# Working on a sublayer's end in two streams of 128 tokens, in the part of the program that handles the latents alone

## The chip, the cores and the metric

The kernel runs on one core of a Trainium2 chip. The time is the device time of one execution in microseconds (us): the median of three runs of the kernel before is 2366.17 us (2364.31 to 2366.91).

## The reference, cut to what matters

Two layers of a backbone work on 256 context tokens and 256 latent tokens, with 1024 channels each. Every layer has three sublayers: a half-step SwiGLU network, four token mixers whose outputs are merged and projected, and a second half-step SwiGLU network. Only the latents are returned, so in the last layer the contexts are needed up to the mixers' inputs and are then dropped.

```python
def rms_norm(x, g):
    y = xf * lax.rsqrt(jnp.mean(xf * xf, axis=-1, keepdims=True) + EPS)
    return (y * g.astype(jnp.float32)).astype(x.dtype)

def ffn_sublayer(x, mod, j, g_pre, g_post, w1, w3, w2):
    h = modulate(rms_norm(x, g_pre), mod[:, :, 3 * j], mod[:, :, 3 * j + 1])
    return x + FFN_RES_WEIGHT * mod[:, :, 3 * j + 2] * rms_norm(swiglu(h, w1, w3, w2), g_post)
...
x_lat = x_lat + mod_lat[:, :, 5] * rms_norm(y_lat, norm_post[layer, 1])
x_lat = ffn_sublayer(x_lat, mod_lat, 2, *ffn_b)
```

Between two sublayers stands, for every token, a norm over the 1024 channels of the first one's output (over all its blocks), the addition to x, and the norm over the sum that the next one begins with.

## The kernel before, in words

Channels lie on the 128 partitions, in 8 blocks, and tokens lie along the free dimension: columns 0 to 255 are the contexts and 256 to 511 the latents. Weights come from memory in pieces of 128 x 1024 (8 blocks of 128 x 128). ScalarE rounds each piece to a high part (`whi`, line 317), VectorE takes the rest as the low part (`wlo`, line 318), and `mm3` (lines 345 to 347) multiplies with three matmuls per block, high by high, high by low and low by high, in the type fp32r. Raw pieces have 3 buffers, split ones 4.

`halves(toks)` lists the streams that lie within a range of tokens: contexts and latents for all 512, and one stream of 256 when the latents are alone. Its callers decide by that list how an end is worked on:

- `post_block` (line 569) takes one finished block of 128 channels: its square, its scaled copy, and, where another sublayer follows, the product with x and the square of the copy. It adds these to three running sums (`sqa`).
- `norms` (line 595) sums them over the partitions with matmuls by a column of ones (`st`, line 303), takes two inverse roots with short VectorE operations (lines 291 to 296), and spreads each over the partitions with a matmul and a copy (`rb`, `rbs`, lines 310 and 312).
- `lead` (line 624) scales the output, adds it to x, and makes the next input `hh`, `hl` block by block (lines 631, 632, 563, 565, 566).
- `turn` (line 636) orders an end. With two streams the last five weight pieces (`skew` = 5) are first used for the first stream, then the norms of that stream are emitted, then the pieces are used for the second stream: four of them still lie split in their buffers, and the first one is loaded and split again. After it come the first stream's `lead`, the second stream's `norms`, the first four pieces of the next sublayer (`ahead`), and the second stream's `lead`. With one stream nothing is held back: all pieces are used for all 256 tokens, and norms and lead follow.
- `ffn` and `mix` read the same list. With two streams, `ffn` runs its first four pieces one stream after the other, and `down` makes separate matmuls for the two streams in the last three output blocks (`m >= KB - 3`). `mix` always uses `halves(ALL_T)` for its own beginning.

The latents are alone from the end of layer 1's mixers (`mix(1, LAT_T, ...)`) through the last network (`ffn(1, 1, LAT_T, ...)`). All engines run the instructions of their queue in order. That order is settled when the program is built, from priorities that follow the order of emission.

Of the kernel before, what the change touches and what calls it, by code (L numbers as in the profile page):

```python
# [7 lines left out]
F32 = mybir.dt.float32  # L8
F32R = mybir.dt.float32r
I32 = mybir.dt.int32  # L10
AF = mybir.ActivationFunctionType
ALU = mybir.AluOpType
# [3 lines left out]
P = 128  # L16
D = 1024
# [8 lines left out]
CTX_T = (0, NCTX)  # L26
LAT_T = (NCTX, NTOK)
# [159 lines left out]
class Kern:  # L187
# [97 lines left out]

    def rsqrt(self, v, shape, tag):
        nc = self.nc
        s = self.small.tile(shape, I32, tag=tag + "s", name=self.nm("rs"))
        y = self.small.tile(shape, F32, tag=tag + "y", name=self.nm("ry"))
        t = self.small.tile(shape, F32, tag=tag + "t", name=self.nm("rt"))  # L290
        nc.vector.tensor_scalar(s, v.bitcast(I32), 1, None, op0=ALU.logical_shift_right)
        nc.vector.tensor_scalar(y.bitcast(I32), s, -1, 0x5F3759DF, op0=ALU.mult, op1=ALU.add)
        for _ in range(3):
            nc.vector.tensor_tensor(t, y, y, op=ALU.mult)
            nc.vector.scalar_tensor_tensor(t, t, -0.5, v, op0=ALU.mult, op1=ALU.mult)
            nc.vector.scalar_tensor_tensor(y, t, 1.5, y, op0=ALU.add, op1=ALU.mult)
        return y
# [177 lines left out]


    def halves(self, toks):
        return [(v, t) for v, t in ((0, CTX_T), (1, LAT_T)) if t[0] >= toks[0] and t[1] <= toks[1]]

    def new_h(self):  # L480
        return [(self.u("hh", F32R, "h"), self.u("hl", F32R, "h")) for _ in range(KB)]
# [87 lines left out]
    def post_block(self, l, s, m, ps, toks, nxt, tag="u"):  # L569

        nc = self.nc
        a, b = toks
        out = self.post
        gp = self.mod[l][3 * s + 2]
        if m not in out["y"]:
            out["y"][m] = self.u("ay")
        y = out["y"][m]

        def add(k, f):
            new = k not in out  # L580
            if new:
                out[k] = self.u("sqa")
            t = out[k] if m == 0 else self.u("sq", tag=tag)
            f(t[:, a:b])
            if m:
                nc.vector.tensor_tensor(out[k][:, a:b], out[k][:, a:b], t[:, a:b], op=ALU.add)  # L586

        add("yy", lambda t: nc.scalar.activation(t, ps[:, a:b], AF.Square))  # L588
        for v, (p, q) in self.halves(toks):
            nc.scalar.activation(y[:, p:q], ps[:, p:q], AF.Identity, scale=gp[:, m, v : v + 1])  # L590
        if nxt:
            add("xa", lambda t: nc.vector.tensor_tensor(t, self.x[m][:, a:b], y[:, a:b], op=ALU.mult))
            add("aa", lambda t: nc.scalar.activation(t, y[:, a:b], AF.Square))

    def norms(self, post, nxt, half):


        nc = self.nc
        v, (a, b) = half
        n = (b - a) // P  # L600

        st = self.ps("st", "h")
        self.stat(st, 0, post["yy"], (a, b))
        if nxt:
            s2 = self.ps("st", "f")
            self.stat(s2, 0, post["aa"], (a, b))
            self.stat(s2, n, post["xa"], (a, b))
        t = self.small.tile([P, n], F32, tag=f"sv{n}", name=self.nm("sv"))
        nc.vector.tensor_scalar(t, st[:, :n], 1.0 / D, EPS, op0=ALU.mult, op1=ALU.add)
        r = self.rsqrt(t, [P, n], f"sr{n}")  # L610
        rs = self.u("rbs", tag="f")
        self.cast(r, n, rs, 0)
        if nxt:
            w = self.small.tile([P, n], F32, tag=f"sx{v}", name=self.nm("sx"))
            nc.vector.tensor_tensor(w, s2[:, :n], r, op=ALU.mult)
            nc.vector.scalar_tensor_tensor(w, s2[:, n : 2 * n], 2.0, w, op0=ALU.mult, op1=ALU.add)
            nc.vector.tensor_tensor(w, w, r, op=ALU.mult)
            nc.vector.scalar_tensor_tensor(w, w, 1.0 / D, self.sx[v], op0=ALU.mult, op1=ALU.add)
            self.sx[v] = w
            r2 = self.rsqrt(w, [P, n], f"sr{n}")  # L620
            self.cast(r2, n, rs, n * P)
        return rs

# [1197 lines left out]
```

## Time and profile before

| | |
|---|---|
| median of 3 runs | 2366.17 us |
| profiled execution | 2369.64 us, of which the span is 2367.8 us |
| TensorE busy, share of the span | 96% |
| VectorE, ScalarE busy | 69%, 38% |
| granted TensorE clock, mean | 0.982 |

The span runs from the first to the last instruction that the profiler recorded; the rest of the profiled execution lies around it. Busy times of TensorE count pipelined matmuls from issue to a modelled end. The start times of two neighbours give their distance.

### The profile page before, as it was taken

The numbers are of one execution on the slowest core, as the hardware profiler recorded it, in microseconds if no ns is written. First come the engines' busy times: TensorE is split into PE (matmuls) and PEld (weight loads), VectorE is DVE, ScalarE is ACT, GpSimd is POOL, SyncE is SP. The second block draws the span as 40 slices with busy tenths as digits, with TensorE's granted clock in tenths as the row PEclk, the third lists the DMA queues.
The fourth block names the chain that finished last, engine by engine and source line by source line (L and its number), as shares of the span: only waits on it lengthen the run. The fifth ranks groups of instructions, "written<-read, shape, count | busy, mean of one in ns | idle before, by whom it ended". The sixth has DMA issues, their size and how long they took to land.

```text
span 2367.8 us, 39296 instructions
## 1 busy us (share of the span) xinstructions
PE 2267.1 (96%) x15428; PEld 1915.7 (81%) x15428; DVE 1635.8 (69%) x4025; ACT 903.0 (38%) x1551; POOL 53.3 (2%) x116
## 2 busy tenths in 40 slices
PE   7999999999999999989999999999998999998997
PEld 4778789987567777878887898888897877898997
DVE  5887675756665574899875478777666886777554
ACT  3322323454443323532332333323244563345442
POOL 0000020000000000000002000000000000000000
PEclk9999999999999999999999999999998999998999
DMA  7545554231541243245554325665532331454663
GB/s 244 172 153 165 184 180 130 75 94 55 171 139 41 85 148 94 72 134 165 180 187 153 98 77 176 180 182 182 182 103 91 113 107 57 161 174 135 185 182 114
DMA packets 105848, 326.82 MB, mean 138 GB/s; under 512 B 16256, under 2 KB 19072, under 8 KB 105664
## 3 DMA queue, kind: packets, MB, share of 16 engines
q1 hardware_dynamic: 97312, 306.52, 42.1%
q0 software_dynamic: 4032, 9.93, 1.2%
q10 hardware_dynamic: 4320, 7.87, 1.0%
q8 instruction: 121, 1.98, 0.3%
q14 instruction: 63, 0.52, 0.1%
HBM read 311.20 MB, written 15.17 MB: 138 GB/s over the span
## 4 chain that ended last, share of the span: by engine, by line
PE 84%; DVE 10%; ACT 3%; DMA 2%; issue 1%; SPq 0%; DVEq 0%; ACTq 0%
PE h L345 11%; PE h L347 11%; PE h L346 11%; PE y L345 6%; PE y L347 6%; PE y L346 6%; PE pj L345 5%; PE pj L347 5%; PE pj L346 5%; PE s L841 2%; DVE wlo L318 2%; DMA araw<-in_w_adaT_dram 1%; PE od L868 1%; ACT whi L317 1%; PE tk L347 1%
## 5 line engine op out<-in xcount | busy, mean ns | idle before, releaser
L317 ACT CAST whi<-raw 128x1024 fp32r<-128x1024 f32 x402 | 421.2, 1050 | 810.4 <-DMA raw<-in_ffn_dram 282.9
L318 DVE TENSOR_TENSOR wlo<-raw,whi 128x1024 fp32r<-128x1024 f32 x402 | 490.7, 1222 | 287.6 <-ACT whi L317 285.5
L345 PE MATMUL h<-hh,whi 128*128 128x512 f32 (+1 forms) x1472 | 528.1, 360 | 12.2 <-DVE gf L686 5.0
L347 PE MATMUL h<-hh,wlo 128*128 128x512 f32 (+1 forms) x1472 | 526.0, 359 | 8.7 <-DVE wlo L318 8.7
L346 PE MATMUL h<-hl,whi 128*128 128x512 f32 (+1 forms) x1472 | 525.7, 358 | 0.0
L345 PEld LDWEIGHTS h<-hh,whi 128*128 128x128 f32 x1472 | 281.8, 192 | 57.6 <-issue 5.3
L347 PEld LDWEIGHTS h<-hh,wlo 128*128 128x128 f32 x1472 | 281.8, 192 | 51.1 <-DVE wlo L318 8.8
L346 PEld LDWEIGHTS h<-hl,whi 128*128 128x128 f32 x1472 | 282.1, 192 | 38.7
L345 PE MATMUL y<-gh,whi 128*128 128x256 f32 (+1 forms) x902 | 290.4, 322 | 2.5 <-ACT t L685 2.5
L347 PE MATMUL y<-gh,wlo 128*128 128x256 f32 (+1 forms) x902 | 291.0, 323 | 0.0
L346 PE MATMUL y<-gl,whi 128*128 128x256 f32 (+1 forms) x902 | 290.5, 322 | 0.0
L345 PE MATMUL pj<-hh,whi 128*128 128x256 f32 (+1 forms) x800 | 276.8, 348 | 3.3 <-ACT hh L565 2.7
L347 PE MATMUL pj<-hh,wlo 128*128 128x256 f32 (+1 forms) x800 | 274.5, 345 | 4.3 <-DVE wlo L318 4.3
L346 PE MATMUL pj<-hl,whi 128*128 128x256 f32 (+1 forms) x800 | 275.7, 346 | 0.4 <-issue 0.4
L345 PEld LDWEIGHTS y<-gh,whi 128*128 128x128 f32 x902 | 171.7, 190 | 15.7 <-ACT t L685 2.7
L347 PEld LDWEIGHTS y<-gh,wlo 128*128 128x128 f32 x902 | 171.7, 190 | 12.9
L346 PEld LDWEIGHTS y<-gl,whi 128*128 128x128 f32 x902 | 171.7, 190 | 12.9
L347 PEld LDWEIGHTS pj<-hh,wlo 128*128 128x128 f32 x800 | 154.2, 194 | 24.7 <-DVE wlo L318 4.9
L345 PEld LDWEIGHTS pj<-hh,whi 128*128 128x128 f32 x800 | 154.2, 194 | 23.6 <-issue 5.2
L346 PEld LDWEIGHTS pj<-hl,whi 128*128 128x128 f32 x800 | 154.5, 194 | 18.4 <-issue 3.9
L424 DVE SCALAR_TENSOR_TENSOR aj<-araw,cr 128x512 f32<-128x512 f32 x112 | 77.0, 687 | 55.9 <-DMA araw<-in_w_adaT_dram 55.7
L586 DVE TENSOR_TENSOR sqa<-sqa,sq 128x256 f32<-128x256 f32 (+1 forms) x154 | 71.6, 493 | 49.9 <-ACT sq L588 49.3
(395 smaller groups left out, 3073.5 us busy)
## 6 DMA issues: line engine op xcount, KB each, us to landing
raw<-in_ffn_dram SPq DMA_DIRECT2D x267, 512.0 KB, 3.8
araw<-in_w_adaT_dram SPq DMA_DIRECT2D x104, 512.0 KB, 4.1
raw<-in_win_dram SPq DMA_DIRECT2D x102, 512.0 KB, 3.7
araw<-in_w_ada_dram SPq DMA_DIRECT2D x24, 512.0 KB, 4.0
raw<-in_wout_dram SPq DMA_DIRECT2D x17, 512.0 KB, 3.5
raw<-in_wbr_dram SPq DMA_DIRECT2D x16, 512.0 KB, 3.6
araw<-in_w_ada_dram SPq DMA_DIRECT2D x22, 256.0 KB, 5.6
s5G<-s5g POOLq DMA_DIRECT2D x16, 256.0 KB, 3.0
```

The source lines that it names most:

```text
L317: self.nc.scalar.copy(hi, src)
L318: self.nc.vector.tensor_tensor(lo, src, hi.bitcast(F32), op=ALU.subtract)
L345: mm(ps, wh, xh, start=start, stop=False, skip_group_check=True)
L346: mm(ps, wh, xl, start=False, stop=False, skip_group_check=True)
L347: mm(ps, wl, xh, start=False, stop=stop, skip_group_check=True)
L424: nc.vector.scalar_tensor_tensor(w if v else junk, w, 1.0, S[v], op0=ALU.mult, op1=ALU.mult, accum_out=t[:, 2 * op + i, v : v + 1])
L586: nc.vector.tensor_tensor(out[k][:, a:b], out[k][:, a:b], t[:, a:b], op=ALU.add)
L841: nc.tensor.matmul(s[:, :w], q[:, j * P : (j + 1) * P], k[:, :w], start=True, stop=True)
L868: nc.tensor.matmul(out[n][64 * h : 64 * h + 64, j * P : (j + 1) * P], vh(kb), ph[:, kb * P : (kb + 1) * P], start=kb == 0, stop=kb == nk - ...
```

## The change

`halves` gives two streams of 128 tokens where the range begins at the latents. `post_block` no longer uses it for choosing the context's or the latent's scale. The small tiles of `norms` and `rsqrt` are made at least two columns wide and cut to the width in use, and the second norm's running sum `sx` is read by the stream's own column.

```diff
     def halves(self, toks):
-        return [(v, t) for v, t in ((0, CTX_T), (1, LAT_T)) if t[0] >= toks[0] and t[1] <= toks[1]]
+
+        mid = (LAT_T[0] + LAT_T[1]) // 2
+        parts = ((1, (LAT_T[0], mid)), (1, (mid, LAT_T[1]))) if toks[0] >= LAT_T[0] else ((0, CTX_T), (1, LAT_T))
+        return [(v, t) for v, t in parts if t[0] >= toks[0] and t[1] <= toks[1]]
...
         add("yy", lambda t: nc.scalar.activation(t, ps[:, a:b], AF.Square))
-        for v, (p, q) in self.halves(toks):
+        for v, (p, q) in ((0, (a, min(b, LAT_T[0]))), (1, (max(a, LAT_T[0]), b))):
+            if p >= q:
+                continue
             nc.scalar.activation(y[:, p:q], ps[:, p:q], AF.Identity, scale=gp[:, m, v : v + 1])
...
-        t = self.small.tile([P, n], F32, tag=f"sv{n}", name=self.nm("sv"))
+        t = self.small.tile([P, 2], F32, tag="sv2", name=self.nm("sv"))[:, :n]
         nc.vector.tensor_scalar(t, st[:, :n], 1.0 / D, EPS, op0=ALU.mult, op1=ALU.add)
-        r = self.rsqrt(t, [P, n], f"sr{n}")
+        r = self.rsqrt(t, [P, n], "sr2")
...
-            w = self.small.tile([P, n], F32, tag=f"sx{v}", name=self.nm("sx"))
+
+            w = self.small.tile([P, 2], F32, tag=f"sx{v if n == 2 else 0}", name=self.nm("sx"))[:, :n]
+            old = self.sx[v] if n == 2 else self.sx[v][:, (a - LAT_T[0]) // P : (a - LAT_T[0]) // P + 1]
...
-            nc.vector.scalar_tensor_tensor(w, w, 1.0 / D, self.sx[v], op0=ALU.mult, op1=ALU.add)
-            self.sx[v] = w
+            nc.vector.scalar_tensor_tensor(w, w, 1.0 / D, old, op0=ALU.mult, op1=ALU.add)
+            if n == 2:
+                self.sx[v] = w
```

## Rows read from the trace of the kernel before

**Rows 1.** The page: busy time of each engine, share of the span, instructions.
```profile
PE 2267.1 (96%) x15428; PEld 1915.7 (81%) x15428; DVE 1635.8 (69%) x4025; ACT 903.0 (38%) x1551; POOL 53.3 (2%) x116
```
**Rows 2.** Windows around mix(1)'s end and the program's end: engines' busy time, clock, DMA.
```profile
core 0: us, PE busy (x) PEld busy (x) DVE busy (x) ACT busy (x) POOL busy (x), PEclk, DMA share, GB/s
2146.00:2166.00 20.00, 9.93 (x46) 9.03 (x45) 17.67 (x64) 6.19 (x13) 0.00 (x0) 0.57 0.19 56
2166.00:2180.00 14.00, 14.00 (x119) 14.00 (x119) 8.45 (x13) 8.37 (x12) 0.00 (x0) 1.00 0.43 117
2180.00:2260.00 80.00, 80.00 (x669) 80.00 (x668) 44.57 (x57) 37.59 (x56) 0.00 (x0) 1.00 0.64 187
2355.00:2368.00 13.00, 1.32 (x6) 0.97 (x5) 7.41 (x28) 0.37 (x1) 0.00 (x0) 0.55 0.24 81
```
**Rows 3.** Timeline of TensorE at mix(1)'s end: start, duration, line, operation [idle, releaser].
```profile
2145.85 0.28 PE L346 MATMUL wo<-ml,whi 128*128 128x256 f32 x1
2145.97 0.28 PE L347 MATMUL wo<-mh,wlo 128*128 128x256 f32 x1
...
2161.58 1.01 PE L345 MATMUL h<-hh,whi 128*128 128x256 f32 x3 [1.52 <-ACT hh L565]
...
2164.96 0.41 PE L345 MATMUL h<-hh,whi 128*128 128x256 f32 x1
2165.17 0.32 PE L346 MATMUL h<-hl,whi 128*128 128x256 f32 x1
2165.33 0.28 PE L347 MATMUL h<-hh,wlo 128*128 128x256 f32 x1
```
**Rows 4.** Timeline of TensorE, two places: 512 columns, then four narrow matmuls of 2 columns.
```profile
526.26 0.39 PE L345 MATMUL pj<-hh,whi 128*128 128x512 f32 x1
526.49 0.39 PE L346 MATMUL pj<-hl,whi 128*128 128x512 f32 x1
...
526.94 1.04 PE L787 MATMUL hs<-cst,sq 128*128 128x2 f32 x8
527.85 0.48 PE L345 MATMUL pj<-hh,whi 128*128 128x512 f32 x1
```
**Rows 5.** Timeline of TensorE: 128 columns in f32, then transposes of 128 columns.
```profile
1874.95 1.13 PE L810 MATMUL hb<-cst,he 128*128 128x128 f32 x8 [0.15 <-DVE he L805]
1875.83 0.36 PE L345 MATMUL pj<-hh,whi 128*128 128x256 f32 x1
...
2101.95 1.06 PE L1578 MATMUL yt<-cst,gl 128*128 128x128 f32 x8
2102.77 0.36 PE L345 MATMUL pj<-hh,whi 128*128 128x256 f32 x1
```
**Rows 6.** Weight loads by shape: count, busy us, mean ns of one, idle before.
```profile
L346 PEld LDWEIGHTS wo<-ml,whi 128*128 128x128 f32 x168 | 31.9, 191 | 1.0
L787 PEld LDWEIGHTS hs<-cst,sq 128*128 128x128 f32 x64 | 8.0, 191 | 2.1 <-ACT sq L900 0.8 <-issue 0.8 <-ACT sq L1205 0.3
L1578 PEld LDWEIGHTS yt<-cst,gl 128*128 128x128 f32 x16 | 1.8, 140 | 0.4 <-issue 0.3
```
**Rows 7.** Timeline at the end of layer 0's mixers, where two streams run: ScalarE, VectorE, TensorE.
```profile
990.16 0.38 ACT L588 ACTIVATE sq<-wo 128x256 f32<-128x256 f32 x1 [1.68 <-PE wo L347]
...
1016.08 1.22 DVE L318 TENSOR_TENSOR wlo<-raw,whi 128x1024 fp32r<-128x1024 f32 x1
...
1017.35 0.58 PE L347 MATMUL h<-hh,wlo 128*128 128x256 f32 x1 [6.52 <-DVE wlo L318]
...
1021.57 0.38 PE L345 MATMUL h<-hh,whi 128*128 128x256 f32 x1
...
1029.93 1.31 ACT L565 ACTIVATE hh<-ht,mod 128x256 fp32r<-128x256 f32 x3 [0.55 <-DVE ht L563]
```
**Rows 8.** VectorE and ScalarE operations by shape, 256 against 128 columns.
```profile
L586 DVE TENSOR_TENSOR sqa<-sqa,sq 128x256 f32<-128x256 f32 x112 | 43.8, 420 | 41.2 <-ACT sq L588 40.8
L1132 DVE TENSOR_TENSOR cx<-cx,ck 128x128 f32<-128x128 f32 x20 | 5.7, 286 | 0.7 <-ACT cx L1130 0.4
L588 ACT ACTIVATE sq<-y 128x256 f32<-128x256 f32 x25 | 9.5, 381 | 46.8 <-PE y L347 46.8
L1130 ACT ACTIVATE cx<-cx 128x128 f32<-128x128 f32 x20 | 6.0, 301 | 3.6 <-DVE cx L1127 3.5
```
**Rows 9.** Timeline of the program's end: TensorE, VectorE, SyncE.
```profile
2353.25 0.28 PE L347 MATMUL y<-gh,wlo 128*128 128x256 f32 x1
2354.55 0.58 PE L303 MATMUL st<-cst,sqa 128*128 128x1 f32 x4 [1.03 <-DVE sqa L586]
2360.40 4.83 SPq L1797 DMA_DIRECT2D out_dram<-x  x8
```
**Rows 10.** DMA issues: source, count, KB each, median us to landing.
```profile
raw<-in_ffn_dram SPq DMA_DIRECT2D x267, 512.0 KB, 3.8
```
**Rows 11.** The page's costliest groups: weight splits, count, busy us, mean ns, idle before.
```profile
L317 ACT CAST whi<-raw 128x1024 fp32r<-128x1024 f32 x402 | 421.2, 1050 | 810.4 <-DMA raw<-in_ffn_dram 282.9
L318 DVE TENSOR_TENSOR wlo<-raw,whi 128x1024 fp32r<-128x1024 f32 x402 | 490.7, 1222 | 287.6 <-ACT whi L317 285.5
```

More of the change, by code (lines that the diff above doesn't have):

```diff
@@ L287, in rsqrt @@
         nc = self.nc
-        s = self.small.tile(shape, I32, tag=tag + "s", name=self.nm("rs"))
-        y = self.small.tile(shape, F32, tag=tag + "y", name=self.nm("ry"))
-        t = self.small.tile(shape, F32, tag=tag + "t", name=self.nm("rt"))
+        w, full = shape[-1], shape[:-1] + [max(shape[-1], 2)]
+        s = self.small.tile(full, I32, tag=tag + "s", name=self.nm("rs"))[..., :w]
+        y = self.small.tile(full, F32, tag=tag + "y", name=self.nm("ry"))[..., :w]
+        t = self.small.tile(full, F32, tag=tag + "t", name=self.nm("rt"))[..., :w]
         nc.vector.tensor_scalar(s, v.bitcast(I32), 1, None, op0=ALU.logical_shift_right)
@@ L617, in norms @@
             nc.vector.tensor_tensor(w, w, r, op=ALU.mult)
-            nc.vector.scalar_tensor_tensor(w, w, 1.0 / D, self.sx[v], op0=ALU.mult, op1=ALU.add)
-            self.sx[v] = w
-            r2 = self.rsqrt(w, [P, n], f"sr{n}")
+            nc.vector.scalar_tensor_tensor(w, w, 1.0 / D, old, op0=ALU.mult, op1=ALU.add)
+            if n == 2:
+                self.sx[v] = w
+            r2 = self.rsqrt(w, [P, n], "sr2")
             self.cast(r2, n, rs, n * P)
```

## The prediction

> **What bounds the kernel now.** The page comes first: TensorE is busy 96% of the span, VectorE 69% [rows 1]. For a kernel so full of matmuls, the question for any edit is how many matmul passes it adds and how much TensorE idle time it fills. Windows come next, laid over the two stretches that the change touches: the end of layer 1's mixers and the program's end. In the steady stretch from 2180 to 2260 TensorE is busy 80.00 of 80 us; from 2146 to 2166 it is busy 9.93 of 20 at a granted clock of 0.57; from 2355 to 2368 it is nearly empty [rows 2]. These two holes are all that a second stream could fill.
>
> The timeline gives the first hole its size. The last mixer projection starts at 2145.97. The first matmul of the next network starts at 2161.58, and until 2165.33 the passes come at 0.21 us instead of 0.12: the clock's lower level, 1.2 GHz, after the wait [rows 3]. Seventeen of the 96 passes of the first four pieces (4 pieces x 8 blocks x 3) start before 2165.33. The other 79 follow at 0.12, so the 96 are issued by 2165.33 + 79 x 0.12 = 2174.8. Without a hole they would be issued by 2146.09 + 96 x 0.12 = 2157.6. **The hole costs 17.2 us.** The second hole is the tail: the span ends 2367.8 - 2353.25 = 14.5 us after the last matmul starts [rows 9].
>
> **What the change adds on TensorE.** Where a matmul of 256 columns becomes two of 128, the number of passes doubles. Counted from the code:
> - mix(1): the last five of eight output blocks, 5 x 8 x 3 = 120 passes become 240.
> - the last network's first four pieces: 96 become 192.
> - its down projection: the blocks m = 5, 6, 7 with 22 inputs each, 3 x 22 x 3 = 198 become 396.
>
> That is 414 extra passes, all in stretches where TensorE is otherwise back to back. So the price of a pass decides. A pass of 256 columns takes 0.12 us [rows 3]; three of 512 take 0.68 from 526.26 to 526.94, 0.227 each [rows 4]: 256 more columns cost 0.107 us, and streaming alone would let 128 columns take 0.120 - 0.053 = 0.067. But each pass also loads 128 columns of weights. That load is recorded at 191 ns for the fp32r pass (`wo`) and the same 191 ns for the f32 pass (`hs`), and at 140 for a transpose [rows 6]. What such a load costs when hardly anything streams is seen in `hs`, 2 columns wide: four f32 matmuls, recorded as eight passes, take from 526.94 to 527.85, 0.114 us a pass [rows 4]. So the load, not the stream, is the floor. From the other side, f32 passes of exactly 128 columns (`hb`) take 0.88 / 8 = 0.110 by their neighbours' starts and (1.13 - 0.28) / 7 = 0.121 by their own span [rows 5]. The trace before has no fp32r pass under 256 columns. I take 0.117, the middle of 0.114 and 0.121, since both rows have the same 191 ns load; outer ends are 0.067 (the load hides) and 0.23 (the narrow fp32r matmul needs two passes, as an f32 one does). **A pass of half the width thus costs what the full one costs**: each split adds 2 x 0.117 - 0.120 = 0.114 us, and 414 of them 47.2 us (44.7 to 50.5 within the inner ends).
>
> The first stream's norms now run between matmuls instead of in the hole: at mix(1) 3 sums and 2 spreads, at the end 1 and 1. At two passes each these are 14 passes of 0.12, **1.7 us**.
>
> A stated rule speaks for a lower price. The Trainium skill, page "TensorE: Matmul & The Clock Gate", section "Back-to-back issue gap", gives about 81 ns per matmul for streams of weight load and matmul at 128 columns; by it 414 x (0.162 - 0.120) = 17.4 us stand in place of 47.2. The rows of 0.110 to 0.121 speak against it here, though no run so far shows this pass itself.
>
> **What it takes away at mix(1).** The first stream's work is over 120 half passes before the second's, so its norms and lead can run under 120 x 0.117 + 1.2 = 15.2 us of matmuls. How long they take is seen where the two streams already run, at the end of layer 0's mixers: the first stream's last evacuation starts at 990.16, and the next network's first matmul only at 1017.35, 27.2 us later. It waited for `wlo` of the next network's first piece, which stands on VectorE behind that stream's lead and the other's post blocks [rows 7]. In that time VectorE does 8 x 4 operations of lead, 5 x 4 of the second stream's blocks and about 4 of the first's last block. At 128 columns each is shorter by 420 - 286 = 134 ns [rows 8], together 56 x 0.134 = 7.5 us; weight splits and the short root operations keep their length. So 27.2 - 7.5 = 19.7 us stand against 15.2 of cover: a wait of 4.5 us, after which the clock is low again. There the 20 passes from 1017.35 to 1021.57 took 4.2 us instead of 2.4 [rows 7], so 1.8 us more. **What remains of the hole: 6.3 us** (bounds 0 and the old 17.2). At the second boundary the second stream's `hh` came 12.6 us after the first matmul in layer 0 [rows 7], here some 2.1 less (16 operations of lead); the 96 half passes last 11.2, and the slow clock's 1.8 adds to that: no wait.
>
> **What it takes away at the end.** The second stream's tail has half the columns: 16 operations of lead save 16 x 0.134 = 2.1 us, square and sum 0.08 + 0.13 [rows 8], sums and spreads two passes less each, 0.5 us, and the copy 0.07. That is **2.9 us** of 14.5; it falls to nothing if the eight output transfers, spaced over 4.83 us now [rows 9], set the end.
>
> **What hides.** The first of the five pieces is loaded and split once more in each end: 3.8 us to landing [rows 10], then 1.05 on ScalarE and 1.22 on VectorE [rows 11]. It waits for one split buffer, free when the second stream's first piece is done (24 x 0.117 = 2.8 us), and is needed after four (11.2 us). On SyncE's queue it stands ahead of the next network's pieces, which are used at half the old pace there. Without that cover it would cost up to 6 us each time. The extra operations of the second stream's post blocks (4 on VectorE, 3 on ScalarE per block) fit into 2.8 us of matmuls per piece. The second root chain, some 30 short operations, lies under the first stream's matmuls at mix(1) and beside the second stream's matmuls at the end. The tiles cut to width and the new loop in `post_block` issue the same instructions elsewhere, at no cost.
>
> **The sum.** 47.2 + 1.7 - 17.2 + 6.3 - 2.9 = **+35.1 us**. The profiled execution's own time is 2369.6, so 2404.7 for it; the median shown is 3.5 us lower, and on it the change gives 2366.2 + 35.1 = **2401 us**. Within the inner ends of the pass and 2 to 11 us of remaining wait the sum goes from +28 to +43, 2394 to 2409.
>
> **Rivals.**
> - *The load hides.* TensorE loads weights for the next pass under the present one, and nothing in the 256-column rows shows the load as a limit. The transposes have a shorter load and come every 0.82 / 8 = 0.10 us [rows 5]. At 0.10 the sum is 414 x 0.080 + 1.7 - 17.2 + 6.3 - 2.9 = +21; at 0.067 it is -6, 2360: faster. It decides below 2p = 0.149, a pass of 0.075. Against it: `hs` pays 0.114 with nothing to stream, and its load is recorded as long as the fp32r one. By the 81 ns of the Trainium skill's page "TensorE: Matmul & The Clock Gate" ("Back-to-back issue gap") this rival's time would be 2371.
> - *The second stream covers nothing.* VectorE is full under the matmuls, as in layer 0, and the hole returns whole at the boundary: +35.1 + 10.9 = +46, 2412. For it speaks that `wlo` stands last in the queue; against it, that the operations are a third shorter.
> - *The narrow fp32r matmul falls back to two passes*, as f32 has them: 414 x (0.46 - 0.12) + 1.7 - 17.2 - 2.9 = +122, 2488. No row shows a narrow fp32r pass, so it can't be excluded; the wait would then be fully covered. Nothing speaks for it either: a 256-column fp32r matmul is one pass at full rate.
>
> **How the numbers follow.** Forecast 0.70, load hides 0.12, no cover 0.10, two passes 0.08. The range of 2380 to 2416 holds nearly all of the forecast and of the second rival, and the dearer quarter of the first: 0.8. A difference of 0.2% is 4.7 us, what a measurement of this kernel can tell. Faster by more comes only from the cheap half of the first rival, 0.06; within it 0.03; slower 0.91.
>
> **What would show it.** `wo`, `h` and `y` matmuls of 128 columns after 2120, 828 of them, at a spacing of 0.114 to 0.121: below 0.075 the forecast fails with its sign, at 0.23 with its size. Between the last `wo` and the first `h` a TensorE wait of 2 to 8 us in place of 15.5, released by a `wlo` or by `hh`. The first `h` no earlier than 2161, since wo itself lasts 14 us longer. From the last `y` to the end 11 to 13 us. Up to 2120 nothing should move by more than a microsecond; if it does, the order of the program has changed elsewhere.

## The result: slower by 3.2%, twice the forecast's loss, and the profile after

The changed kernel takes 2443.44 us (median of 4 runs, 2438.43 to 2448.05), the kernel before beside it 2366.54: a ratio of 1.0315, with a 95% interval of 1.0299 to 1.0330, or +75 us (+71 to +78). Forecast were +35 and 2401 us, with a range that ended at 2416. The sign was right and the size was not.

The page gives the engines' busy time, share and instructions, to be read against [rows 1]:

```profile
PE 2354.7 (96%) x15842; PEld 2001.8 (82%) x15842; DVE 1651.4 (68%) x4137; ACT 912.0 (37%) x1585; POOL 53.3 (2%) x116
```

TensorE has 15842 - 15428 = 414 recorded instructions more, the number counted, and stays 96% busy. What the 414 don't explain is how long they took. The windows over the changed stretches show it (busy time and instructions of TensorE, weight loads, VectorE, ScalarE, GpSimd, then granted clock, DMA share, GB/s), beside [rows 2]:

```profile
2135.60:2148.00 12.40, 12.40 (x113) 12.40 (x113) 9.77 (x27) 7.18 (x20) 0.00 (x0) 1.00 0.55 171
2151.00:2176.70 25.70, 25.30 (x119) 25.13 (x119) 18.47 (x75) 10.37 (x26) 0.00 (x0) 0.50 0.26 81
2176.70:2220.70 44.00, 43.57 (x204) 43.22 (x204) 17.69 (x69) 10.49 (x21) 0.00 (x0) 0.50 0.15 48
2220.70:2224.00 3.30, 3.30 (x22) 3.30 (x22) 1.98 (x3) 1.35 (x2) 0.00 (x0) 0.69 0.02 9
2224.00:2230.00 6.00, 6.00 (x53) 6.00 (x52) 2.99 (x4) 2.69 (x4) 0.00 (x0) 1.00 0.55 178
2376.50:2407.50 31.00, 31.00 (x281) 31.00 (x279) 7.65 (x10) 7.52 (x14) 0.00 (x0) 1.00 0.23 74
2411.40:2434.00 22.60, 22.60 (x109) 22.60 (x107) 4.76 (x18) 1.85 (x4) 0.00 (x0) 0.50 0.00 0
```

The reader is to look at TensorE's busy time and at the clock together. From 2151 to 2220 TensorE is busy for 68.9 of 69.7 us, and the clock is 0.50 throughout, the lower of its two levels, 1.2 GHz. The same happens from 2411 to 2434. From 2376 to 2407 equally narrow passes run at 1.00. A busy TensorE thus says nothing of the pace: 281 instructions in 31 us at one level, 109 in 22.6 at the other.

TensorE's timeline (start, duration, line, operation, idle time before and its releaser) shows where the clock falls and where it returns:

```profile
2148.79 0.28 PE L347 MATMUL wo<-ml,whi 128*128 128x128 f32 x1
2148.91 0.28 PE L348 MATMUL wo<-mh,wlo 128*128 128x128 f32 x1
2149.54 0.38 PE L304 MATMUL st<-cst,sqa 128*128 128x1 f32 x2 [0.36 <-DVE sqa L590]
...
2150.58 0.61 PE L304 MATMUL st<-cst,sqa 128*128 128x1 f32 x4 [0.15 <-DVE rs L292]
2151.04 0.42 PE L347 MATMUL wo<-ml,whi 128*128 128x128 f32 x1
2151.26 0.42 PE L348 MATMUL wo<-mh,wlo 128*128 128x128 f32 x1
...
2176.51 0.41 PE L348 MATMUL wo<-mh,wlo 128*128 128x128 f32 x1
2176.73 0.41 PE L346 MATMUL h<-hh,whi 128*128 128x128 f32 x1
...
2220.53 0.41 PE L348 MATMUL h<-hh,wlo 128*128 128x128 f32 x1
2220.75 0.52 PE L346 MATMUL h<-hh,whi 128*128 128x256 f32 x1
...
2222.56 0.38 PE L348 MATMUL h<-hh,wlo 128*128 128x256 f32 x1
2222.78 0.29 PE L346 MATMUL h<-hh,whi 128*128 128x256 f32 x1
2222.90 0.28 PE L347 MATMUL h<-hl,whi 128*128 128x256 f32 x1
...
2407.49 0.27 PE L348 MATMUL y<-gh,wlo 128*128 128x128 f32 x1
2408.12 0.38 PE L304 MATMUL st<-cst,sqa 128*128 128x1 f32 x2 [0.36 <-DVE sqa L590]
...
2410.88 0.79 PE L311 MATMUL rb<-cst,ry 128*128 128x128 f32 x2 [1.20 <-DVE ry L297]
2411.32 0.45 PE L347 MATMUL y<-gl,whi 128*128 128x128 f32 x1
...
2433.97 0.41 PE L348 MATMUL y<-gh,wlo 128*128 128x128 f32 x1
2435.08 0.59 PE L304 MATMUL st<-cst,sqa 128*128 128x1 f32 x2 [0.69 <-DVE sqa L590]
```

A narrow pass takes 0.111 us before the first sum (as do the 279 y passes from 2376.49 to 2407.49), and 0.213 from 2151.04 on. It stays at 0.213 for 69.7 us, until the first passes of 256 columns: nine of these come at 0.21, the next at 0.12. At the last network's end, ten passes behind the first sum still come fast; the clock falls around the wait of 1.20. In the kernel before, too, the clock had fallen in the hole [rows 3], but what followed it was 256 wide, and it was back within 4 us.

In time, between landmarks of the two profiled executions (before / after, us; of the kernel before, the first pass of a stretch is counted back at 0.12 from its last):

| stretch | before | after | difference |
|---|---|---|---|
| five wo blocks and the wait, to the first h | 29.9 | 41.1 | +11.2 |
| first four h pieces | 13.2 | 44.0 | +30.8 |
| h and y of 256 columns | 154.8 | 155.7 | +0.9 |
| last three y blocks | 23.6 | 57.5 | +33.8 |
| last y to the end of the span | 14.5 | 12.1 | -2.4 |

That is +74.3. The span's other 4.0 lie ahead of the first stretch, where the two programs do the same work. It begins at 2135.7 here, but in two experiments below at 2131.6 and 2131.8, as before (2131.7), and in run 6, which is the kernel before up to there, the last wo comes 2.9 late: the 4 us are a spread between executions. The forecast's sign that nothing up to 2120 would move by more than a microsecond can't be read from single profiles.

### The profile page after: what moved, and what is told of

It is laid out like the page before. It is cut to its first block, busy times and chain, and to the rows that moved or that the text cites. A ratio compares the mean times of both kernels' runs of the same rounds, so it can differ in the third digit from the quotient of the medians.

```text
span 2446.1 us, 40283 instructions
## 1 busy us (share of the span) xinstructions
PE 2354.7 (96%) x15842; PEld 2001.8 (82%) x15842; DVE 1651.4 (68%) x4137; ACT 912.0 (37%) x1585; POOL 53.3 (2%) x116
## 4 chain that ended last, share of the span: by engine, by line
PE 78%; DVE 13%; DMA 5%; ACT 2%; issue 2%; DVEq 0%; ACTq 0%
PE h L346 9%; PE h L348 9%; PE h L347 9%; PE y L348 6%; PE y L346 6%; PE y L347 6%; PE pj L346 5%; PE pj L348 5%; PE pj L347 5%; DVE wlo L319 3%; DMA araw<-in_w_adaT_dram 2%; PE s L850 2%; DMA raw<-in_ffn_dram 1%; ACT whi L318 1%; PE wo L347 1%
## 5 line engine op out<-in xcount | busy, mean ns | idle before, releaser
L346 PE MATMUL h<-hh,whi 128*128 128x512 f32 (+2 forms) x1504 | 544.8, 363 | 10.8 <-DVE gf L695 5.1
L348 PE MATMUL h<-hh,wlo 128*128 128x512 f32 (+2 forms) x1504 | 543.5, 362 | 7.9 <-DVE wlo L319 7.9
L347 PE MATMUL h<-hl,whi 128*128 128x512 f32 (+2 forms) x1504 | 542.7, 362 | 0.0
L347 PEld LDWEIGHTS h<-hl,whi 128*128 128x128 f32 x1504 | 296.5, 197 | 38.7
L346 PE MATMUL y<-gh,whi 128*128 128x256 f32 (+2 forms) x968 | 312.9, 323 | 2.5 <-ACT t L694 2.5
L348 PE MATMUL y<-gh,wlo 128*128 128x256 f32 (+2 forms) x968 | 313.6, 324 | 0.0
L347 PE MATMUL y<-gl,whi 128*128 128x256 f32 (+2 forms) x968 | 313.1, 323 | 0.0
L346 PEld LDWEIGHTS y<-gh,whi 128*128 128x128 f32 x968 | 189.3, 196 | 15.6 <-ACT t L694 2.7
L347 PEld LDWEIGHTS y<-gl,whi 128*128 128x128 f32 x968 | 189.4, 196 | 13.0
L348 PEld LDWEIGHTS y<-gh,wlo 128*128 128x128 f32 x968 | 189.4, 196 | 12.9
L590 DVE TENSOR_TENSOR sqa<-sqa,sq 128x256 f32<-128x256 f32 (+2 forms) x172 | 74.0, 459 | 70.2 <-ACT sq L592 69.4
```

The lines of the kernel that those rows point to most:

```text
L346: mm(ps, wh, xh, start=start, stop=False, skip_group_check=True)
L347: mm(ps, wh, xl, start=False, stop=False, skip_group_check=True)
L348: mm(ps, wl, xh, start=False, stop=stop, skip_group_check=True)
```

## The experiments

Theory: in these stretches TensorE's clock, once fallen, stays low under passes of 128 columns and comes back under passes of 256 or 512. Rival at first: the clock is low there for another reason (the norms, the end as a whole), and width has no part in it. Later: what makes it fall. The diffs show only the lines that carry the edit. A difference from the changed kernel is that of the two ratios to the kernel before, times 2366 us.

**1. Narrow passes alone.** One stream as before; only the passes are halved.

```diff
+        if narrow:
+            for c in (slice(0, P), slice(P, 2 * P)):
+                self.mm3(ps[:, c], w, (xh[:, c], xl[:, c]), start, stop)
+            return
...
-  ..., kb == 0, kb == KB - 1)
+  ..., kb == 0, kb == KB - 1, toks == LAT_T and m >= 3)
```

> The kernel before, with one stream, in which the same 414 matmul passes of 256 columns are each made as two of 128: the last five blocks of wo, the first four pieces of the last network, the last three blocks of its down projection. Norms, lead and the order of the ends stay as before. Theory (TensorE's clock, once fallen to 1.2 GHz, stays there while the passes are 128 columns wide and returns with 256-wide ones; the changed kernel shows narrow passes at 0.213 us at the low level and 0.111 at the full one): the 15 us wait between wo and h stays, after it all 192 narrow h passes come at 0.213 = 41 us instead of the 13.2 that the 96 wide ones took, +28; wo at the full clock 240 x 0.111 - 120 x 0.120 = +12; y at the full clock 396 x 0.111 - 198 x 0.120 = +20; sum +60, about 2427 us. Rival (the clock is low for those 71 us for another reason, such as the norms between the matmuls, and narrow passes bring it back as wide ones do): +42 plus some 2, about 2410 us, with h at 0.111 after some 4 us.

Here the two halves' sums alternate in one bank, and the output is not the reference's; only the time of the passes is read. Measured: 2457.97 us, ratio 1.0373 (1.0352 to 1.0393). The condition on the tokens also held for layer 0's second stream, which was not meant: 120 passes more are split there, and the stretch of mix(1) begins 28.9 us late. From there to the end it takes 2458.8 - 2160.6 = 298.2 us, before 236.1: **+62, as the theory said** (+60), not +42. Windows of layer 0's end, wo, h and y:

```profile
1000.00:1040.00 40.00, 40.00 (x189) 40.00 (x189) 19.18 (x44) 12.22 (x25) 0.00 (x0) 0.50 0.16 53
2160.60:2186.90 26.30, 26.30 (x238) 26.30 (x237) 14.95 (x30) 11.24 (x23) 0.00 (x0) 1.00 0.44 140
2202.10:2243.00 40.90, 40.89 (x192) 40.89 (x192) 10.22 (x20) 8.70 (x14) 0.00 (x0) 0.50 0.12 39
2400.30:2444.40 44.10, 44.10 (x398) 44.10 (x396) 7.65 (x9) 7.49 (x11) 0.00 (x0) 1.00 0.13 41
```

With no norm step among them, 240 wo and 396 y passes of 128 columns run at the full clock to their last one. The h passes, which begin after the old hole, stay at the low one for all 192, and so do the unintended ones of layer 0, among which the first stream's norms stand. There the clock fell at 995.8, behind three short waits of TensorE (0.54, 0.30, 0.13).

**2. Only mix(1)'s end and the first h pieces in two streams.**

```diff
-        parts = (...) if toks[0] >= LAT_T[0] else (...)
+        parts = (...) if toks[0] >= LAT_T[0] and self.two else (...)
...
+        if toks == LAT_T:
+            self.two, hv = False, [(1, LAT_T)]
```

> The changed kernel with two streams only at the end of mix(1) and in the first four pieces of the last network; the network's down projection and its end run in one stream of 256, as before. Theory: of the cost, 216 extra passes at the full clock's price 216 x 0.102 = 22, and 113 wo and 192 h passes at the low clock 305 x 0.102 = 31; less the 17 us hole; some 2 to 5 of norm passes and short waits: +38 to +41 against the kernel before, about 2405 us, and the changed kernel's remaining +36 to +39 lies at the last network's end. Rival (the clock's part belongs to the end as a whole, or the hole did not really close): +6 to +10 if the low clock does not show up here, about 2374.

Measured: 2414.26 us, 1.0185 (1.0165 to 1.0206), +44 (+39 to +49), where +38 to +41 were expected; wo and h run as in the changed kernel (clock 0.50 from 2150 to 2219), and y, 256 wide, at 1.00. The other end thus costs the remaining 0.013, 31 us, as the table's 33.8 - 2.4. Each end has its own slow stretch.

**3. The first h pieces 256 wide.**

```diff
-        for _, rng in hv if ws else ():
+        for _, rng in ([(1, toks)] if toks == LAT_T else hv) if ws else ():
```

> The changed kernel, except that the first four pieces of the last network run 256 columns wide (96 passes) after both streams' leads. Theory: the hole between wo and h comes back in part (norms and lead of a 128-token stream after the last wo: some 11 to 14 us), and the wide passes bring the clock back within some 4 us (20 passes at 0.21, 76 at 0.12 = 13.3 us): 13 + 13.3 = 26 us in place of the 40.9 that 192 narrow passes took at 0.213; about -14 against the changed kernel, about 2429 us. Rival (the low clock lasts its time whatever the width of the passes): 13 + 96 x 0.21 = 33 us and the pieces behind them at the low clock too, so within 5 us of the changed kernel or above it.

Measured: 2423.35 us, 1.0227 (1.0205 to 1.0248), 21 us less than the changed kernel; expected were 14 less. A hole of 12.3 us is back (2175.95 to 2188.27), yet hole and 96 wide passes take 25.4 us where the narrow ones took 44.2. The windows of the hole and of what follows it:

```profile
2176.30:2188.20 11.90, 3.23 (x11) 2.43 (x10) 9.11 (x50) 2.59 (x8) 0.00 (x0) 0.50 0.13 45
2188.30:2192.00 3.70, 3.70 (x18) 3.70 (x19) 3.46 (x14) 2.09 (x7) 0.00 (x0) 0.54 0.00 0
2192.00:2201.00 9.00, 9.00 (x77) 9.00 (x76) 4.77 (x6) 5.49 (x8) 0.00 (x0) 1.00 0.25 74
```

An idle TensorE for 12 us was cheaper here than one busy with narrow passes at the low clock.

**4. Wide passes in between.** After the last spread of each stream's norms, ScalarE makes an operand from it, and TensorE runs 12 passes of 512 columns whose result nobody reads.

```diff
+        if n == 1:
+            self.warm(rs[:, (n * P if nxt else 0) : (n * P if nxt else 0) + P], 12)
```

> The changed kernel plus 12 matmuls of 512 columns, whose results nobody reads, behind the last spread of each stream's norms, four places in all (after 127 of 240 wo passes, in the first h passes, after 272 of 396 y passes, and behind the last y). Each copy of their operand waits for the norms as the spread does. Theory: the wide passes bring the clock back to 2.4 GHz after each group's 4 to 5 us, and the narrow passes behind them run at 0.111 instead of 0.213: some 365 of the 429 slow ones x 0.102 = -37, less three groups of 12 x 0.23 to 0.45 us = 8 to 15: -22 to -29 against the changed kernel, about 2418 us. Rival (the clock does not answer to the width of the passes): the groups only cost, +12 to +20, about 2458 us.

Measured: 2424.87 us, 1.0234 (1.0219 to 1.0249), 19 less than the changed kernel. The timeline at the first group shows narrow wo passes on either side of it:

```profile
2153.92 0.41 PE L354 MATMUL wo<-ml,whi 128*128 128x128 f32 x1
2154.13 0.41 PE L355 MATMUL wo<-mh,wlo 128*128 128x128 f32 x1
2154.59 4.45 PE L320 MATMUL dm<-dk 128*128 128x512 f32 x12
...
2159.27 0.27 PE L354 MATMUL wo<-ml,whi 128*128 128x128 f32 x1
2159.38 0.28 PE L355 MATMUL wo<-mh,wlo 128*128 128x128 f32 x1
```

The same kind of pass comes at 0.213 before the group and at 0.111 behind it: the theory holds, the rival's +12 to +20 doesn't. The saving is under the 22 to 29 expected: 331 passes became fast and not 365, and the three groups ahead of the last y took 13.4 us, near the upper end of 8 to 15. In h the second stream's sums made TensorE wait again (1.26 us, up to 2171.19), and the clock was low from there to the next group.

**5. What makes it fall: the last network's norm steps later.** The same instructions; the first stream's sum stands one weight piece further back, its spread one more.

```diff
+            if late and k == 0:
+                st = self.ps("st", "h")
+                self.stat(st, 0, post["yy"], hv[0][1])
+            if late and k == 1:
+                rs = self.norms(post, nxt, hv[0], st)
```

> The changed kernel with the same instructions, but at the last network's end the first stream's sum stands one weight piece later among TensorE's matmuls (24 narrow passes) and its spread two pieces after the stream's last block, so that their inputs are ready when their turn comes. In the changed kernel TensorE waited 0.36 us before that sum and 1.20 before that spread, then the clock fell and the remaining 124 narrow y passes came at 0.213. Theory (it is TensorE's wait between narrow passes after which the clock falls): no wait, all 396 y passes at 0.111, last y 12 us earlier against the first narrow y: -12 against the changed kernel, about 2434 us. Rival (the sum of one column and the spread make it fall whether or not they wait): no difference beyond 2 us.

Measured: 2427.42 us, 1.0257 (1.0230 to 1.0285), 14 less; all 396 y passes are fast, and their stretch takes 45.4 us in place of 57.5, -12.1. TensorE still waits 0.66 before the spread (no wait was expected), and the clock stays at 1.00, as it does there in runs 7 and 8. So here the sum, the spread and one such wait don't lower it. In the changed kernel, where TensorE waited 0.36 and 1.20 for them, it fell.

**6. The kernel before, with its hole filled.**

```diff
         self.cast(r, n, rs, 0)
+        if self.fillup == 1:
+            self.warm(rs, 8)
```

> The kernel before with 8 matmuls of 512 columns that nobody reads between the two spreads of mix(1)'s end, where TensorE waits 4.7 us. Theory: the wide passes bring the clock up before the next network starts, so its first 17 passes take 0.12 instead of 0.21 (-1.8 us) and the second spread about 0.4 less; the group needs 8 x 0.41 = 3.3 us of the 3.5 that are free after its operand's copy: -2 to -3 us, 2366, which a measurement can hardly tell from the kernel before. Rival: the group makes the second spread late by its own length's excess, +1 to +3.

Measured: 2366.01 us, 0.9999 (0.9985 to 1.0014): no difference that can be told; the expected -2 to -3 lies within that interval. The 8 passes took 3.64 us and did raise the clock (the spread behind them 0.68 us long, not 1.20), but TensorE then waited 1.52 for `hh`, and behind six faster h passes the next came at 0.21 again, from 2164.97 to 2167.96.

**7. All norm steps later.**

```diff
             work(i, w, hv[1])
+            if alone and go:
+                try:
+                    next(go)
+                except StopIteration as e:
+                    rs, go = e.value, None
```

> The changed kernel with the same instructions, but each norm step of the streams of 128 (sums, first spread, second spread) stands one weight piece after the step that it waits for: for the first stream of mix(1)'s end among the second stream's wo passes, for the second stream among the first stream's h passes, at the last network's end as in the run beside this one. Theory (the clock falls after TensorE's short waits and then stays low under narrow passes): without those waits it stays up through wo (240 x 0.111 + 1.6 = 28 us in place of 41.0, -13), h (192 x 0.111 + 2 = 23.4 in place of 44.0, -20) and y (-12); the second stream's lead comes later and its first h pieces wait 2 to 6 us: -39 to -45 in all, about 2402 us, which is what the blind forecast gave without a slow clock. Rival (the norm's small matmuls make the clock fall by themselves, or narrow passes do): within 5 us of the changed kernel.

Measured: 2422.35 us, 1.0237 (1.0211 to 1.0263), 18 less than the changed kernel where 39 to 45 were expected. The y stretch gained its 12; wo gained 6.5 of the 13 expected and h 0.9 of 20. In wo one wait was left, at the first spread (timeline, then windows):

```profile
2153.03 0.49 PE L312 MATMUL rb<-cst,ry 128*128 128x128 f32 x2 [0.95 <-DVE ry L298]
...
2154.98 0.32 PE L347 MATMUL wo<-mh,whi 128*128 128x128 f32 x1
2155.10 0.42 PE L348 MATMUL wo<-ml,whi 128*128 128x128 f32 x1
2155.31 0.42 PE L349 MATMUL wo<-mh,wlo 128*128 128x128 f32 x1
```
```profile
2167.50:2210.50 43.00, 43.00 (x203) 43.00 (x203) 20.55 (x74) 11.37 (x23) 0.00 (x0) 0.50 0.18 61
2210.60:2220.00 9.40, 9.40 (x70) 9.40 (x70) 4.94 (x7) 4.03 (x6) 0.00 (x0) 0.87 0.34 115
```

Two microseconds after a single wait of 0.95 the passes slow down, and then 43.00 us of h without any wait stay at 0.50. The expectation missed the one wait. Its rival (within 5 us) doesn't hold either. On the theory that narrow passes don't bring the clock back, this row and run 1's h are the cleanest: no idle time, and no return before the 256-wide passes.

**8. The same, with wide passes ahead of each spread.** The edit is shown against run 7.

```diff
         yield
+        self.wide(14)
         self.cast(r, n, rs, 0)
```

> The kernel of the run before (the changed kernel with its norm steps later) plus 68 matmuls of 256 columns that nobody reads, in five groups of 12 to 16, each directly ahead of a spread of a 128-token stream at mix(1)'s end or among the first h passes, and ahead of the second stream's first h. There TensorE would otherwise wait some 1 us (0.95 before the first spread in the run before, behind which the clock stayed low through 43 us of narrow h passes without any wait). Theory (the slow clock is the one term that the forecast lacked, and it needs a wait between narrow passes to begin): the clock stays at 2.4 GHz through wo, h and y; wo about 31 us and h about 28 instead of 34.4 and 43.1 in the run before, -18 against it, about 2404 us, which is the blind forecast's sum plus some 3 for the filling. Rival (narrow passes let the clock fall sooner or later also without a wait): low clock in wo or h again, and a time within 8 us of the run before, 2422, or above it by the 8 us that the filling takes.

Measured: 2421.31 us, 1.0233 (1.0203 to 1.0264), not to be told from run 7; expected were 18 less. The profiled execution is the shortest of its four (2416.62). In it wo took 30.6 us at 1.00 (31 expected) and y 45.4, but h 38.7, not 28:

```profile
2133.30:2163.90 30.60, 30.60 (x275) 30.60 (x273) 24.33 (x91) 14.13 (x38) 0.00 (x0) 1.00 0.35 106
2164.00:2169.00 5.00, 4.82 (x25) 4.17 (x24) 4.21 (x16) 3.99 (x10) 0.00 (x0) 0.75 0.25 94
2169.00:2172.30 3.30, 0.23 (x2) 0.04 (x1) 3.27 (x8) 2.18 (x6) 0.00 (x0) 0.50 0.34 104
2172.30:2179.00 6.70, 6.52 (x30) 6.44 (x31) 4.89 (x30) 0.00 (x0) 0.00 (x0) 0.50 0.30 105
2185.70:2202.60 16.90, 16.90 (x152) 16.90 (x151) 9.64 (x25) 8.39 (x16) 0.00 (x0) 1.00 0.20 62
```

The timeline shows where the clock fell:

```profile
2164.46 0.33 PE L348 MATMUL h<-hl,whi 128*128 128x128 f32 x1 [0.17 <-DVE hl L571]
...
2166.37 0.30 PE L347 MATMUL h<-hh,whi 128*128 128x128 f32 x1
2166.62 0.47 PE L348 MATMUL h<-hl,whi 128*128 128x128 f32 x1
2166.89 0.41 PE L349 MATMUL h<-hh,wlo 128*128 128x128 f32 x1
2167.11 0.41 PE L347 MATMUL h<-hh,whi 128*128 128x128 f32 x1
...
2172.34 1.74 PE L305 MATMUL st<-cst,sqa 128*128 128x1 f32 x6 [3.11 <-DVE sqa L591]
```

With wo at the full clock TensorE reaches h sooner than VectorE has made `hl`. Its passes then come three at a time, one block about every 0.54 us, with one recorded wait of 0.17; from 2166.5 on they take 0.21. The second stream's sums also come too soon: VectorE is still busy (3.27 of 3.30 us), and TensorE waits 3.11 us, which the slow clock had covered before. That wait began at 2169.2, behind the fall, and so didn't cause it. The outcome is what the rival said, a low clock in h again and a time within 8 us of run 7. A fall thus needs no long wait. Whether narrow passes fed without any pause would fall too, this run doesn't show; in run 1 they didn't for 44 us.

## Why the prediction was wrong

**The step that failed: the price of a pass, taken at the full clock everywhere but behind "a wait of 4.5 us, after which the clock is low again ... so 1.8 us more".** It took the 20 slow passes of layer 0 [rows 7] as the price of a fall of the clock. Those passes were 256 wide, and what was to run behind the waits here was 128 wide. A fall was foreseen at the first h alone; that the clock would not come back was not. In wo and y, where the norms stand as 14 passes of 0.12 and nothing else, neither a wait nor a fall was foreseen. Measured in its place: no wait ahead of the first h, and 412 narrow passes (113 wo, 192 h, 107 y; the fourth expectation's 429 counted 17 too many) at 0.213 instead of 0.111: 412 x 0.102 = **42.0 us**, 19.6 of them in h and 22.4 in wo and y. The rows of before showed it nowhere, since no narrow fp32r stretch followed a wait in them; at layer 0's end the same norm steps stand between 256-wide passes, and the clock stayed at 1.00 there (991.0 to 1002.5). That the clock does not come back under the narrow passes is shown by runs 1, 3, 4 and 7.

**The wait before h (4.5 forecast) was 0.** In the changed kernel the last `hh` of the first stream starts 14.7 us after that stream's last evacuation (2148.88 to 2163.57), where the forecast took 19.7 from layer 0; TensorE needs them one block at a time. The 27.2 us behind that 19.7 is misread: 1017.35 is the first pass by `wlo`. The next network's first passes, by `whi`, came 17.0 us after the evacuation:

```profile
1007.20 0.28 PE L345 MATMUL h<-hh,whi 128*128 128x256 f32 x1
```

The slow wo passes gave cover as well. In run 8, with wo at the full clock, the first 13 h passes, paced by `hl`, took 2.4 us where 1.3 would do, and TensorE waited 3.11 for the second stream's sums, a wait that the forecast didn't have.

**The number of the passes was right, and so, nearly, was their price at the full clock.** 414 more, at 0.111 rather than 0.117: 414 x (0.222 - 0.120) = 42.2 us, forecast 47.2. So a floor that hardly depends on the columns holds, as `hs` and `hb` suggested [rows 4, 5], and the rival's 0.067 and 0.10 are out. That the load is this floor fits the rows; no run isolates it. The Trainium skill's page "TensorE: Matmul & The Clock Gate", section "Back-to-back issue gap", gives about 81 ns for such a pair of load and matmul; this fp32r pass measures 111 ns at the full clock and 213 at the low one, and the measurement decides. That 213 is near the third rival's 0.23 is chance: it is one pass at half the clock, since 289 of the same y passes run at 0.111.

**The hole went (-17.2), and the tail shrank by 2.4** (forecast 2.9), with 12.1 us from the last y to the end, inside the 11 to 13 named [rows 9].

The sum with the measured terms: 42.2 + 42.0 - 17.2 - 2.4 = 64.6 of 74.3. The rest is the ten norm steps between narrow passes, 4.3 us by their starts where 1.7 were forecast (the second stream's four in h, 2.1 us, were not counted), six short waits of TensorE, 2.9 together, and 0.9 of slow 256-wide passes: 8.1. Some 1.6 us are not assigned. Without the clock the forecast's form would have come to 42.2 + 1.7 - 17.2 - 2.4 = +24, under its +35: the dearer pass and the feared wait hid part of the missing term.

No version tried beats the kernel before. The reason is in the first term: even at the full clock the splits cost 42 us, more than hole and tail together are worth (17.2 + 14.5).

What stays open is what makes the clock fall among narrow passes. It fell behind waits of 0.36 and 0.15 us (wo) and around one of 1.20 (y) in the changed kernel, behind 0.54, 0.30 and 0.13 (run 1, layer 0), behind 0.95 (run 7), and behind 0.17 where the passes were paced by `hl` (run 8); behind one of 0.66 it did not (runs 5, 7, 8). The length of one wait doesn't sort these.

## What to carry to other kernels

Halving a matmul's columns at a full pass price can cost twice, once in passes and once in clock: price the narrow stretch at both clock levels, and ask what the first wide pass after it is. When work is put into a hole, read the granted clock beside the busy share; 43 us of uninterrupted busy time ran at half the clock here. And a slow engine hides the waits that come next: what is won on it uncovers them, as at `hl` and at the sums in run 8.

## What the runs showed of the hardware that was not expected

- At the full clock an fp32r pass of 128 columns takes 0.111 us and one of 256 takes 0.12; at the low clock both take 0.213. The narrow one gains 0.01 us or nothing by its width.
- Narrow passes without waits kept the full clock where they had it (44.1 us of y at 1.00 in run 1) and did not regain it once it was lost (43.00 of 43.00 us busy at 0.50 in run 7); a group of 12 passes of 512 columns brought it back within its 4.45 us (run 4).
- In the kernel before, filling a wait of TensorE with wide passes gained nothing that can be told (0.9999): the clock rose, and fell again behind a later wait of 1.52 us (run 6).
- A fall needs no long wait: in run 8 the clock fell among narrow passes behind a recorded wait of 0.17 us, where they came three about every 0.54 us.
